# A hybrid decoder trunk on one core: PSUM evictions of the FFN groups at a higher scheduling priority, three of four joined blocks written back one product later

## The chip, the cores and the metric

The kernel runs on one core of a Trainium2 chip. The metric is device time in microseconds (us) of the whole program, from one launch; three runs of the kernel before give a median of 2379.33 us (2377.66 to 2384.99). A profile of one execution gives the times of single instructions. The engines have short names in it: PE is TensorE (matmul), PEld its weight load, DVE is VectorE, ACT is ScalarE, POOL is GpSimd, SP is SyncE, whose queue starts the DMAs.

## The reference

Two layers (DEPTH = 2) act on x of 512 tokens by 1024 features. Each layer is a half-step SwiGLU FFN, a mixing block of three gated branches (stick-breaking attention, forgetting attention, memory cross-attention), and a second half-step FFN, each with an RMS norm before and after. All is float32. The change touches the FFN alone:

```python
def _swiglu(t, w_gate, w_up, w_down):
    return (jax.nn.silu(t @ w_gate) * (t @ w_up)) @ w_down

f = _swiglu(_rmsnorm(h, ffn1_pre_g[l]), ffn1_w_gate[l], ffn1_w_up[l], ffn1_w_down[l])
h = h + 0.5 * _rmsnorm(f, ffn1_post_g[l])
...
f = _swiglu(_rmsnorm(h, ffn2_pre_g[l]), ffn2_w_gate[l], ffn2_w_up[l], ffn2_w_down[l])
h = h + 0.5 * _rmsnorm(f, ffn2_post_g[l])
```

The hidden width D_FF is 2816, that is 22 tiles of 128.

## The kernel before, in words

**Stages.** The program runs FFN a0, mixing, FFN c0 (layer 0), then FFN a1, mixing, FFN c1 (layer 1). Names of tiles carry these letters: `pwa0g` is a PSUM bank of the token-major gate products of a0, `pdc` one of the down products of c0 or c1, `wh_da` a weight of the down group of a0 or a1.

**Three matmuls for one.** A float32 operand is kept as an upper part and a rest (`h` and `l`); `split` (line 179) makes the upper part by a copy on ACT (line 182, or 185 with a scale) and the rest by a subtraction on DVE (line 183 or 186). `mm3` (line 203) adds three matmuls into one bank: upper by upper (205), upper by rest (206), rest by upper (207). Each weight tile thus needs a DMA into a `raw` tile, a cast on ACT and a subtraction on DVE before PE can use it. The tiles `wh` and `wl` have four buffers each (`BUFS`, line 102), and a product of the groups below uses two of each.

**Seven products for eight.** Sixteen of the 22 hidden tiles are computed token-major, in two column halves `ci` = 0 and 1, in groups of seven products in place of eight block products (a Winograd form of Strassen's scheme). `token_product` (line 740) is one such product of gate or up; the groups are called G0, U0, G1 and U1 here. Weights of the seven products are blocks or differences of blocks of the weight (`BlockUnit`, line 274; the difference is made on DVE at line 327). The products run in `ORDER` (0, 2, 1, 3, 4, 5, 6). `SUM` says into which of three pairs of PSUM banks a product adds: pair 0 takes products 0, 3, 5 and 6, pair 1 takes 1, pair 2 takes 2 and 4. Pair 1 starts as a copy of pair 0 after product 0 (line 747). A pair is read between the products that add to it, and a product may add to its pair only when the reading before it is done; products 5 and 6 follow each other directly on pair 0.

**Reading out.** At the end of a product its two banks are read: copies on ACT for products 2 and 3 (line 775), additions on DVE for 4 and 5 (line 777), for 1 and 6 a multiplication by the gate on DVE in the up groups (line 779) or a Silu on ACT in the gate groups (line 781). After 4 and 5 follow a product of whole tiles on DVE (line 784) or a Silu on ACT (line 786).

**Joined blocks.** After products 1, 4, 5 and 6 of an up group one block of the hidden tensor is ready, but token-major; the down group needs it the other way round. `turns` (line 788) collects these blocks, and `turn` (line 790), called four times in each later product, works on them: in the first product after, two copies of 16-bit halves on ACT (line 800) and two transposing DMAs on SP (line 801); when the block has age 2, two copies on ACT (line 804) join the halves in the hidden tensor. The blocks of products 1 and 5 take their planes from the tag `rs`, which has one buffer, the others from the five temporaries (line 99).

**The down group.** `product` (line 851) runs fourteen products of the same kind in the order `DOWN` (line 849), for both column halves into the same banks, so that they are read only after the second half (lines 875 to 886; line 878 copies pair 0 to pair 1). Each factor on the left is made one product ahead by `first_factor` (line 829) from the joined blocks. Eight plain gate and up products of the hidden tiles 18 to 21 stand between the down products (`PLAN`, line 1643).

**What sets the order.** The jobs form a queue (`Queue`); when a job begins, the weights of the jobs after it are loaded and split, four units ahead (`load_ahead`, line 391; a product has two units), so splits stand early in the program. A scheduler of the language then orders the instructions of each engine: among those that it reckons ready when an engine falls free, it takes the one with the best priority, which without further word is its place in the program. On the chip every engine works through its own list in that order.

Of the kernel before, what the change touches and what calls it, by code (L numbers as in the profile page):

```python
# [13 lines left out]
AF = mybir.ActivationFunctionType  # L14
ALU = mybir.AluOpType
# [8 lines left out]
def kernel(  # L24
# [38 lines left out]
    nc = tc.nc  # L63
# [35 lines left out]
    def tmp(name):  # L99
        return sb.tile([P, S], F32, tag="f32t", bufs=5, name=name)  # L100
# [3 lines left out]
    def stile(shape, tag, name, dt=F32R):  # L104
        return sb.tile(shape, dt, tag=tag, bufs=BUFS[tag], name=name)
# [4 lines left out]
    def pbank(tag, name):  # L110
        return ps.tile([P, S], F32, tag=tag, bufs=4, name=name)
# [91 lines left out]
    def mm3(pt, lh, ll, rh, rl, start, stop, free=False):  # L203

        nc.tensor.matmul(pt, lh, rh, start=start, stop=False, skip_group_check=free)  # L205
        nc.tensor.matmul(pt, lh, rl, start=False, stop=False, skip_group_check=free)  # L206
        nc.tensor.matmul(pt, ll, rh, start=False, stop=stop, skip_group_check=free)  # L207
# [261 lines left out]
    HF = (slice(0, S), slice(S, D))  # L469
# [128 lines left out]
    ORDER = (0, 2, 1, 3, 4, 5, 6)  # L598
    SUM = (0, 1, 2, 0, 2, 0, 0)
    TO = ((0, 0), (0, 0), (1, 1), (0, 1), (0, 1), (1, 1), (1, 0))  # L600
    park = [nc.dram_tensor(f"park{i}", (NT, P, D), F32, kind="Internal").ap() for i in range(2 * L)]

    def ffn(l, src, wg, wu, wd, dst, name, spare, parked, plan, aside=None):
# [6 lines left out]
        hid, st = {}, {}  # L610
        hr, turns = {}, []
# [122 lines left out]
        def in_product(n):  # L734
            if n in (0, 1, 6):
                i, j = ((0, 0), (0, 1), None, None, None, None, (1, 1))[n]
                return [block(i, j, part) for part in range(2)]
            return st["u", n]

        def token_product(ci, up, n, uns):  # L740

            nm = f"{name}{'gu'[up]}_{ci}_{n}"
            if n in (0, 1, 2):
                st["c", n] = [pbank("z" if n == 0 else "mm", f"pw{nm}_{e}") for e in range(2)]
            if n == 1:
                for e in range(2):
                    nc.scalar.copy(st["c", 1][e][:], st["c", 0][e][:])
            if n == 0:
                if not up:
                    st["s", ci] = {}  # L750
            pts = st["c", SUM[n]]
            h, l = in_product(n)
            opens, ends = n in (0, 2), n in (1, 4, 6)
            for un in uns:
                for e in range(2):
                    c = slice(e * P, (e + 1) * P)
                    for k in range(un.nk):
# [12 lines left out]
            r = hidden_rows(2 * ci + q[1])[:, :, HALVES[q[0]]] if up else g  # L770
            for e in range(2):
                p = pts[e][:].rearrange("p (f q) -> p f q", f=2)
                re, ge = r[:, 2 * e:2 * e + 2], g[:, 2 * e:2 * e + 2]
                if n in (2, 3):
                    nc.scalar.copy(re, p)
                elif n in (4, 5):
                    nc.vector.tensor_tensor(re, re, p, ALU.add)
                elif up:
                    nc.vector.tensor_tensor(ge, p, ge, ALU.mult)
                else:  # L780
                    nc.scalar.activation(re, p, AF.Silu)
            if n in (4, 5):
                if up:
                    nc.vector.tensor_tensor(g, r, g, ALU.mult)
                else:
                    nc.scalar.activation(r, r, AF.Silu)
            if up and n in (1, 4, 5, 6):
                turns.append([nm, g, (2 * ci + q[1], q[0]), n in (1, 5), 0, None])

        def turn(kk):  # L790

            for one in turns:
                nm, g, (row, i), own, age, planes = one
                if kk == 1 and age == 0:
                    one[5] = planes = ([stile([P, 2, 2 * S], "rs", "tr" + nm, U16)[:, h] for h in range(2)] if own else
                                       [tmp(f"tr{nm}_{h}")[:].bitcast(U16) for h in range(2)])
                    words = g.rearrange("p f q -> p (f q)").bitcast(U16)
                    for h, plane in enumerate(planes):
                        part = tmp(f"th{nm}_{h}")[:].bitcast(U16)
                        nc.scalar.copy(part, words[:, h::2])  # L800
                        nc.sync.dma_start_transpose(plane.rearrange("p (r q) -> p r q", q=P), part)
                if kk in (0, 1) and age == 2:
                    r = hidden_rows(row)[:].bitcast(U16)
                    nc.scalar.copy(r[:, :, i * S + kk:(i + 1) * S:2].rearrange("p f (e q) -> p e f q", e=2),
                                   planes[kk].rearrange("p (e f q) -> p e f q", e=2, q=P))
                if kk == ND // 2 - 1:
                    one[4] += 1
            turns[:] = [one for one in turns if one[4] < 3]

        def token_products(ci, up):  # L810

# [39 lines left out]
        def product(at, uns):  # L851
            ci, n = DOWN[at]
            first, last = ci == 0, ci == NC - 1
            if at == 0:
                RINGS["o"] = 2
                dst.begin()
            if at + 1 < len(DOWN):
                first_factor(*DOWN[at + 1])
            if first and n in (0, 2):
                st["b", SUM[n]] = [pbank("z", f"pd{name}_{n}_{e}") for e in range(2)]  # L860
            pts = st["b", SUM[n]]
            h, l = st.pop(("a", ci, n))
# [12 lines left out]
            if n == 0:  # L875
                st["b", 1] = [pbank("z", f"pd{name}_1_{e}") for e in range(2)]
                for e in range(2):
                    nc.scalar.copy(st["b", 1][e][:], pts[e][:])
                return
            i, hf = TO[n]  # L880
            for e in range(2):
                f = dst.fs[2 * i + e][:, HF[hf]]
                if n in (4, 5):
                    nc.vector.tensor_tensor(f, f, pts[e][:], ALU.add)
                else:
                    nc.scalar.copy(f, pts[e][:])

        def products():

# [768 lines left out]
    for l in LAYERS:  # L1658
        i, mn = 3 * l, []
# [44 lines left out]
```

## Time and profile before

| | us |
|---|---|
| median of three runs | 2379.33 |
| lowest and highest run | 2377.66, 2384.99 |
| the profiled execution, its time | 2378.89 |
| its span in the profile | 2377.2 |
| DVE busy | 1805.5 (76%) |
| ACT busy | 1515.2 (64%) |
| PE, granted clock over the span | 0.999 of full |

The profiled execution lies 0.44 us below the median, and 1.7 us of its time lie outside the span. "Busy" of PE includes time in which a matmul that has begun is drawn out; the ends of matmuls are modelled. A row of the timeline gives the start, the duration, the engine, the line of the kernel, the operation, the tiles written and read, the shape, and in brackets the idle time of the engine just before with what ended it. A row of the waits gives the engine and line that waited, whom it waited for, and the us in total, the times and the longest.

### The profile page before, as it was taken

The numbers are of one execution on the slowest core, as the hardware profiler recorded it, in microseconds if no ns is written. First come the engines' busy times: TensorE is split into PE (matmuls) and PEld (weight loads), VectorE is DVE, ScalarE is ACT, GpSimd is POOL, SyncE is SP. The second block draws the span as 40 slices with busy tenths as digits, with TensorE's granted clock in tenths as the row PEclk, the third lists the DMA queues.
The fourth block names the chain that finished last, engine by engine and source line by source line (L and its number), as shares of the span: only waits on it lengthen the run. The fifth ranks groups of instructions, "written<-read, shape, count | busy, mean of one in ns | idle before, by whom it ended". The sixth has DMA issues, their size and how long they took to land.

```text
span 2377.2 us, 31155 instructions
## 1 busy us (share of the span) xinstructions
PE 2348.8 (99%) x11719; PEld 1982.8 (83%) x11719; DVE 1805.5 (76%) x2358; ACT 1515.2 (64%) x2306; POOL 76.0 (3%) x134
## 2 busy tenths in 40 slices
PE   9999999999999999999999999999999999999998
PEld 7777889888888888778888878888888888887787
DVE  8876877667777689778788778766777767897785
ACT  6777565577766556775557665655777664666744
POOL 0000000000111000000000000000001100000000
PEclk9999999999999999999999999999999999999999
DMA  5666455223223556664647664532323235576643
GB/s 199 194 176 182 159 190 151 75 81 94 86 75 107 186 178 177 185 186 142 230 134 208 182 177 161 199 110 71 98 72 98 80 116 200 160 203 171 194 145 141
DMA packets 299754, 354.98 MB, mean 149 GB/s; under 512 B 78266, under 2 KB 192978, under 8 KB 299604
## 3 DMA queue, kind: packets, MB, share of 16 engines
q1 hardware_dynamic: 299508, 352.97, 48.3%
q8 instruction: 92, 1.51, 0.3%
q14 instruction: 58, 0.48, 0.1%
q0 software_dynamic: 96, 0.03, 0.0%
HBM read 319.39 MB, written 16.78 MB: 141 GB/s over the span
## 4 chain that ended last, share of the span: by engine, by line
PE 84%; DVE 5%; DMA 5%; ACT 4%; issue 2%; SPq 0%; POOL 0%; DVEq 0%; ACTq 0%
PE pg L206 4%; PE pg L205 4%; PE pg L207 4%; PE pda L206 2%; PE pda L207 2%; PE pdc L206 2%; PE pda L205 2%; PE pdc L207 2%; PE pdc L205 2%; PE pb L207 1%; PE pb L206 1%; PE pb L205 1%; DMA raw_da<-in_ffn_w_down_dram 1%; PE pq L206 1%; PE pq L205 1%
## 5 line engine op out<-in xcount | busy, mean ns | idle before, releaser
L205 PE MATMUL pg<-us_a,wh_wg 128*128 128x512 f32 x384 | 150.9, 393 | 0.0
L207 PE MATMUL pg<-us_a,wl_wg 128*128 128x512 f32 x384 | 149.8, 390 | 0.0
L206 PE MATMUL pg<-us_a,wh_wg 128*128 128x512 f32 x384 | 149.8, 390 | 0.0
L206 PE MATMUL pda<-wl_da,aha 128*128 128x512 f32 x224 | 87.8, 392 | 3.5 <-DVE wl_da L183 3.5
L206 PE MATMUL pdc<-wl_dc,ahc 128*128 128x512 f32 x224 | 87.9, 392 | 3.0 <-DVE wl_dc L183 3.0
L205 PE MATMUL pdc<-wh_dc,ahc 128*128 128x512 f32 x224 | 86.8, 390 | 1.4 <-ACT wh_dc L182 1.3
L205 PE MATMUL pda<-wh_da,aha 128*128 128x512 f32 x224 | 86.7, 390 | 1.1 <-ACT wh_da L182 1.1
L207 PE MATMUL pdc<-wh_dc,alc 128*128 128x512 f32 x224 | 87.2, 389 | 0.0
L207 PE MATMUL pda<-wh_da,ala 128*128 128x512 f32 x224 | 87.2, 389 | 0.0
L183 DVE TENSOR_TENSOR wl_da<-raw_da,wh_da 128x1024 fp32r<-128x1024 f32 x50 | 60.9, 1223 | 34.3 <-ACT wh_da L182 34.3
L207 PEld LDWEIGHTS pg<-us_a,wl_wg 128*128 128x128 f32 x384 | 72.1, 188 | 15.2
L183 DVE TENSOR_TENSOR wl_dc<-raw_dc,wh_dc 128x1024 fp32r<-128x1024 f32 x50 | 61.0, 1222 | 30.5 <-ACT wh_dc L182 30.4
L205 PEld LDWEIGHTS pg<-us_a,wh_wg 128*128 128x128 f32 x384 | 72.1, 188 | 14.1
L206 PEld LDWEIGHTS pg<-us_a,wh_wg 128*128 128x128 f32 x384 | 72.2, 188 | 14.1
L182 ACT CAST wh_da<-raw_da 128x1024 fp32r<-128x1024 f32 x50 | 52.2, 1050 | 47.0 <-PE pda L207 16.6
L182 ACT CAST wh_dc<-raw_dc 128x1024 fp32r<-128x1024 f32 x50 | 52.3, 1050 | 43.5 <-PE pdc L207 17.6
L186 DVE SCALAR_TENSOR_TENSOR wl_wg<-raw_wg,wh_wg 128x1024 fp32r<-128x1024 f32 x48 | 58.4, 1220 | 22.2 <-ACT wh_wg L185 22.2
L200 DVE SCALAR_TENSOR_TENSOR ga<-pg,bgate,ga 128x512 f32<-128x512 f32 x48 | 35.9, 747 | 50.0 <-ACT ga L199 50.0
L185 ACT ACTIVATE wh_wg<-raw_wg 128x1024 fp32r<-128x1024 f32 x48 | 50.6, 1058 | 24.7 <-PE pv L1096 11.7
L183 DVE TENSOR_TENSOR wl_uc<-raw_uc,wh_uc 128x1024 fp32r<-128x1024 f32 x44 | 53.7, 1220 | 16.5 <-ACT wh_uc L182 16.5
L182 ACT CAST wh_uc<-raw_uc 128x1024 fp32r<-128x1024 f32 x44 | 46.1, 1050 | 30.7 <-PE pgc L206 7.6
L183 DVE TENSOR_TENSOR wl_ua<-raw_ua,wh_ua 128x1024 fp32r<-128x1024 f32 x44 | 53.6, 1219 | 15.0 <-ACT wh_ua L182 15.0
(647 smaller groups left out, 8053.7 us busy)
## 6 DMA issues: line engine op xcount, KB each, us to landing
raw_da<-in_ffn_w_down_dram SPq DMA_DIRECT2D x66, 512.0 KB, 4.4
raw_dc<-in_ffn_w_down_dram SPq DMA_DIRECT2D x66, 512.0 KB, 4.2
raw_ga<-in_ffn_w_gate_dram SPq DMA_DIRECT2D x52, 512.0 KB, 4.3
raw_ua<-in_ffn_w_up_dram SPq DMA_DIRECT2D x52, 512.0 KB, 4.4
raw_gc<-in_ffn_w_gate_dram SPq DMA_DIRECT2D x52, 512.0 KB, 4.1
raw_uc<-in_ffn_w_up_dram SPq DMA_DIRECT2D x52, 512.0 KB, 3.6
raw_wg<-in_w_gate_dram SPq DMA_DIRECT2D x48, 512.0 KB, 3.5
raw_wo<-in_w_out_dram SPq DMA_DIRECT2D x24, 512.0 KB, 3.4
```

The source lines that it names most:

```text
L182: both = [nc.scalar.copy(h_ap, src)]
L183: make = lambda: nc.vector.tensor_tensor(l_ap, src, h_ap.bitcast(F32), ALU.subtract)
L185: both = [nc.scalar.activation(h_ap, src, AF.Copy, scale=scale)]
L186: make = lambda: nc.vector.scalar_tensor_tensor(l_ap, src, scale, h_ap.bitcast(F32), ALU.mult, ALU.subtract)
L200: nc.vector.scalar_tensor_tensor(t, z, minus, t, ALU.max, ALU.add)
L205: nc.tensor.matmul(pt, lh, rh, start=start, stop=False, skip_group_check=free)
L206: nc.tensor.matmul(pt, lh, rl, start=False, stop=False, skip_group_check=free)
L207: nc.tensor.matmul(pt, ll, rh, start=False, stop=stop, skip_group_check=free)
```

## The change

Three things are edited. The instructions that read PSUM in `token_product` and in `product` are traced inside `tc.high_priority(offset=300)`, which moves their priority 300 places ahead of their place in the program. A block that waits to be joined carries an age of its own, `back`: 2 for the second of the four blocks in ORDER (product 4), 3 for the others (products 1, 5 and 6), where it was 2 for all. Which blocks take their planes from `rs` is now written by their place in ORDER; these are products 1 and 5 as before.

```diff
             if n == 1:
                 for e in range(2):
+                  with tc.high_priority(offset=300):
                     nc.scalar.copy(st["c", 1][e][:], st["c", 0][e][:])
...
-            for e in range(2):
-                p = pts[e][:].rearrange("p (f q) -> p f q", f=2)
...
+            with tc.high_priority(offset=300):
+                for e in range(2):
+                    p = pts[e][:].rearrange("p (f q) -> p f q", f=2)
+                    re, ge = r[:, 2 * e:2 * e + 2], g[:, 2 * e:2 * e + 2]
+                    if n in (2, 3):
+                        nc.scalar.copy(re, p)
+                    elif n in (4, 5):
+                        nc.vector.tensor_tensor(re, re, p, ALU.add)
+                    elif up:
+                        nc.vector.tensor_tensor(ge, p, ge, ALU.mult)
+                    else:
+                        nc.scalar.activation(re, p, AF.Silu)
+                if n in (4, 5):
+                    if up:
+                        nc.vector.tensor_tensor(g, r, g, ALU.mult)
+                    else:
+                        nc.scalar.activation(r, r, AF.Silu)
             if up and n in (1, 4, 5, 6):
-                turns.append([nm, g, (2 * ci + q[1], q[0]), n in (1, 5), 0, None])
+                at = [n for n in ORDER if n in (1, 4, 5, 6)].index(n)
+                turns.append([nm, g, (2 * ci + q[1], q[0]), at % 2 == 0, 0, None, 2 if at == 1 else 3])
...
-                nm, g, (row, i), own, age, planes = one
+                nm, g, (row, i), own, age, planes, back = one
...
-                if kk in (0, 1) and age == 2:
+                if kk in (0, 1) and age == back:
...
-            turns[:] = [one for one in turns if one[4] < 3]
+            turns[:] = [one for one in turns if one[4] <= one[6]]
...
+            with tc.high_priority(offset=300):
+                if n == 0:
+                    st["b", 1] = [pbank("z", f"pd{name}_1_{e}") for e in range(2)]
+                    for e in range(2):
+                        nc.scalar.copy(st["b", 1][e][:], pts[e][:])
+                    return
+                i, hf = TO[n]
                 for e in range(2):
-                    nc.scalar.copy(st["b", 1][e][:], pts[e][:])
-                return
-            i, hf = TO[n]
-            for e in range(2):
-                f = dst.fs[2 * i + e][:, HF[hf]]
-                if n in (4, 5):
-                    nc.vector.tensor_tensor(f, f, pts[e][:], ALU.add)
-                else:
-                    nc.scalar.copy(f, pts[e][:])
+                    f = dst.fs[2 * i + e][:, HF[hf]]
+                    if n in (4, 5):
+                        nc.vector.tensor_tensor(f, f, pts[e][:], ALU.add)
+                    else:
+                        nc.scalar.copy(f, pts[e][:])
```

More of the change, by code (lines that the diff above doesn't have):

```diff
@@ L770, in token_product @@
             r = hidden_rows(2 * ci + q[1])[:, :, HALVES[q[0]]] if up else g
-            for e in range(2):
-                p = pts[e][:].rearrange("p (f q) -> p f q", f=2)
[L773 to L779, printed above, removed]
-                else:
-                    nc.scalar.activation(re, p, AF.Silu)
-            if n in (4, 5):
[L783 to L786, printed above, removed]
+            with tc.high_priority(offset=300):
[15 more added lines that the diff above has]
+                        nc.scalar.activation(r, r, AF.Silu)
             if up and n in (1, 4, 5, 6):
-                turns.append([nm, g, (2 * ci + q[1], q[0]), n in (1, 5), 0, None])
+                at = [n for n in ORDER if n in (1, 4, 5, 6)].index(n)
+                turns.append([nm, g, (2 * ci + q[1], q[0]), at % 2 == 0, 0, None, 2 if at == 1 else 3])
         def turn(kk):
             for one in turns:
-                nm, g, (row, i), own, age, planes = one
+                nm, g, (row, i), own, age, planes, back = one
                 if kk == 1 and age == 0:
@@ L874, in product @@
                 return
-            if n == 0:
-                st["b", 1] = [pbank("z", f"pd{name}_1_{e}") for e in range(2)]
-                for e in range(2):
-                    nc.scalar.copy(st["b", 1][e][:], pts[e][:])
-                return
-            i, hf = TO[n]
-            for e in range(2):
-                f = dst.fs[2 * i + e][:, HF[hf]]
-                if n in (4, 5):
-                    nc.vector.tensor_tensor(f, f, pts[e][:], ALU.add)
-                else:
-                    nc.scalar.copy(f, pts[e][:])
+            with tc.high_priority(offset=300):
[5 more added lines that the diff above has]
+                i, hf = TO[n]
+                for e in range(2):
+                    f = dst.fs[2 * i + e][:, HF[hf]]
[3 more added lines that the diff above has]
+                        nc.scalar.copy(f, pts[e][:])
         def products():
```

## The prediction

> **What bounds the kernel now.** I read the page's first part, then the waits of PE, then the timelines of PE, DVE and ACT around the longest waits.
>
> ```profile
> span 2377.2 us, 31155 instructions
> ...
> PE   9999999999999999999999999999999999999998
> ```
>
> PE is busy for 2348.8 of 2377.2 us, so 28.4 us of the span is all that any reordering can win. The change touches the token-major groups and the down group of the four FFN stages. Four windows hold these (60 to 330, 880 to 1200, 1218 to 1525 and 2055 to 2345 us); their sum row:
>
> ```profile
> sum 1187.00, PE 1169.84 PEld 959.67 DVE 945.91 ACT 767.29 POOL 5.39; mean PE 292.46 PEld 239.92 DVE 236.48 ACT 191.82 POOL 1.35
> ```
>
> In them PE is not busy for 1187.00 - 1169.84 = 17.2 us. That is the ceiling, 0.7% of the time. The waits of PE say whom it waits for (us in total, times, longest):
>
> ```profile
> PE pda L206 <- DVE wl_da L183: 3.5, 4, 1.3
> PE pdc L206 <- DVE wl_dc L183: 3.0, 4, 0.8
> PE pwa0u L205 <- ACT wh_ga L182: 2.0, 1, 2.0
> PE pdc L205 <- ACT wh_dc L182: 1.3, 1, 1.3
> PE pda L205 <- ACT wh_da L182: 1.1, 1, 1.1
> PE pwc1u L206 <- DVE wl_uc L183: 0.8, 1, 0.8
> PE pwa0u L206 <- DVE wl_ua L183: 0.8, 1, 0.8
> PE pwa1u L206 <- DVE wl_ua L183: 0.6, 1, 0.6
> PE pwa0u L205 <- ACT wh_ua L182: 0.5, 1, 0.5
> PE pwc1u L205 <- ACT wh_uc L182: 0.5, 1, 0.5
> PE pwc0u L206 <- DVE wl_uc L183: 0.4, 1, 0.4
> ```
>
> The reader is to see what is missing as much as what is there. Nearly all of it is a wait for a weight: L182 makes the upper part `wh` on ACT, L183 the lower part `wl` on DVE. An eviction out of PSUM hardly appears by name. These eleven rows make 14.5 us. To see why weights are late I went to where it happens. In the first FFN stage, at the end of the second gate group (G1):
>
> ```profile
> 151.68 0.39 PE L207 MATMUL pwa0g<-wh_ga,ula 128*128 128x512 f32 x1
> 152.58 0.50 PE L205 MATMUL pwa0u<-wh_ua,us_x 128*128 128x512 f32 x1 [0.51 <-ACT wh_ua L182]
> ...
> 154.43 0.50 PE L205 MATMUL pwa0g<-wh_ga,us_x 128*128 128x512 f32 x1
> ```
>
> The row at 151.68 is the last matmul of G1's product 5. The next one should belong to product 6 (`pwa0g`), but PE turns to two matmuls of the next group (`pwa0u`), whose weight is not there, and comes to product 6 at 154.43. Products 5 and 6 use the same pair of banks (SUM is 0 for both) and stand next to each other in ORDER, so product 6 may start only when line 777 has read product 5 out. The scheduler found that eviction later than the end of product 5 and filled the hole with work that on the chip is late. What DVE did:
>
> ```profile
> 150.41 1.22 DVE L183 TENSOR_TENSOR wl_ga<-tga,wh_ga 128x1024 fp32r<-128x1024 f32 x1
> 152.56 1.22 DVE L183 TENSOR_TENSOR wl_ua<-raw_ua,wh_ua 128x1024 fp32r<-128x1024 f32 x1 [0.93 <-ACT wh_ua L182]
> 153.70 1.28 DVE L777 TENSOR_TENSOR sa<-sa,pwa0g 128x512 f32<-128x512 f32 x2
> ```
>
> After `wl_ga` it idles 0.93 us for the next weight, splits it, and only then evicts, although product 5 ended at 151.9. **The wait is written on a weight; its root is the eviction's place in DVE's order.** The same at the end of U1, where the down group follows:
>
> ```profile
> 190.62 0.39 PE L207 MATMUL pwa0u<-wh_ua,ula 128*128 128x512 f32 x1
> ...
> 191.98 0.39 PE L207 MATMUL pwa0u<-wh_ua,ula 128*128 128x512 f32 x1
> 193.49 0.49 PE L205 MATMUL pda<-wh_da,aha 128*128 128x512 f32 x1 [1.12 <-ACT wh_da L182]
> ...
> 195.55 0.40 PE L205 MATMUL pwa0u<-wh_ua,us_x 128*128 128x512 f32 x1
> ```
>
> ```profile
> 192.26 1.22 DVE L183 TENSOR_TENSOR ala<-hra,aha 128x1024 fp32r<-128x1024 f32 x1
> 193.47 1.23 DVE L183 TENSOR_TENSOR wl_da<-raw_da,wh_da 128x1024 fp32r<-128x1024 f32 x1
> 194.61 1.28 DVE L777 TENSOR_TENSOR hra<-hra,pwa0u 128x512 f32<-128x512 f32 x2
> ```
>
> Six matmuls lie between the starts 190.62 and 191.98: 0.227 us each, so 24 make a product of 5.44 us.
>
> **The change part by part.** It adds and removes no instruction. The evictions of lines 747, 775 to 786 and 878 to 886 get a better place when the scheduler has several ready instructions for one engine. It can't take one that isn't ready.
>
> (a) End of U1, four times. Product 5 ends at 191.98 + 0.23 = 192.21 and product 6 starts at 195.55 with four matmuls of the down group (0.91 us) between: 2.43 us lost. If line 777 takes the place of `wl_da` at 193.47, its first half (0.64 of 1.28 us) is done at 194.11, and 1.90 us are lost. Gain 0.53, four times: 2.1 us. The split that is pushed back serves the down group, which now starts a product (5.44 us) later; that covers its 1.28 us. Were the cover gone, it would cost these 1.28 us each time.
>
> (b) End of G1, four times. Product 5 ends at 151.91, product 6 starts at 154.43, two matmuls (0.45) lie between: 2.07 us lost. With line 777 right after `wl_ga`, at 150.41 + 1.14 (1.14 is the step from 193.47 to 194.61), product 6 starts at about 152.2 and loses 0.3 us: gain 1.7. The rows of the waits for U groups (0.8, 0.8, 0.6, 0.5, 0.5, 0.4) make 3.6 us, this place 0.51 + 0.8 of it, so all four gain 1.7 x 3.6 / 1.3 = 4.7 us. That needs an eviction that is ready when DVE falls free. Two slipped matmuls, 0.45 us, say that the scheduler saw it less than one DVE operation late: perhaps it wasn't ready, and then priority does nothing. Bounds 0 and 4.7; I take two thirds, 3.1, as four slipped matmuls at (a) show that being taken late for want of priority is common.
>
> (c) End of U0 in layer 0, where PE waited for line 777 behind a split:
>
> ```profile
> 110.88 0.39 PE L207 MATMUL pwa0u<-wh_ua,ula 128*128 128x512 f32 x1
> 113.24 0.47 PE L205 MATMUL pwa0u<-wh_ua,us_x 128*128 128x512 f32 x1 [1.97 <-ACT wh_ga L182]
> ```
>
> ```profile
> 111.27 1.22 DVE L183 TENSOR_TENSOR wl_ua<-tua,wh_ua 128x1024 fp32r<-128x1024 f32 x1 [0.37 <-ACT wh_ua L182]
> ```
>
> If line 777 stands where `wl_ua` stands, its first half ends at 111.27 + 0.64 = 111.91 against a start of product 6 at 113.24: gain 1.3. The row names ACT, which ended last by the profile. Bounds 0 (the order stays) and 2.1 (no wait at all: 113.24 - 110.88 - 0.23); I take 1.3.
>
> (d) The clock. In c1, the last FFN stage, the hand-over of (b) is followed by a drop:
>
> ```profile
> 150.00:160.00 10.00, 8.63 (x36) 6.36 (x35) 6.51 (x8) 5.65 (x6) 0.00 (x0) 1.00 0.80 255
> 2168.00:2176.00 8.00, 7.14 (x22) 5.31 (x23) 3.89 (x5) 3.12 (x4) 0.00 (x0) 0.79 0.69 211
> ```
>
> At a granted 0.79 over 8 us, PE lost some 0.21 x 8 = 1.7 us; after the same stall in the first stage the clock stayed at 1.00. Bounds 0 and 1.7; I take half, 0.8. [...]
>
> (e) The joins (line 804). Three of four blocks per up group come one product later in the program: 8 groups x 3 x 2 copies. None is added. What they cost now is that they stand in ACT's order while their transfer is in flight:
>
> ```profile
> 183.80 1.35 ACT L804 COPY hra<-tra0u 128x1024 uint16<-128x1024 uint16 x1 [2.87 <-DMA tra0u<-tha0u]
> ...
> 185.96 0.58 ACT L775 COPY hra<-pwa0u 128x512 f32<-128x512 f32 x1
> ```
>
> ```profile
> ACT hrc L804 <- DMA trc0u<-thc0u: 9.0, 6, 2.1
> ```
>
> The copy at 183.80 held ACT for 2.87 us, with casts and an eviction behind it. But it runs in product 4, while the program has it in product 5: the scheduler takes a join as soon as its own reckoning says that the data is there. A later place in the program need not move it, so I take 0. Bounds: if it moves, the weights of the hand-overs come earlier, up to what (a) and (c) leave, (4 x 1.90) + 0.8 = 8.4 us; if it hurts, see the third rival. The first joined block of U1 (product 1) is needed by the second down product, two products (10.9 us) after product 6 begins; moved from product 5 to product 6 it keeps about one product of cover, which would cost up to 5.44 us if it were gone. The tag `rs` has one buffer and line 795 makes a tile of it for each plane, so an own block's second transpose waits for its first join, and SP's loads queue behind that transpose.
>
> (f) The down group's own waits:
>
> ```profile
> 223.13 0.50 PE L206 MATMUL pda<-wl_da,aha 128*128 128x512 f32 x1 [0.63 <-DVE wl_da L183]
> ...
> 1062.49 0.50 PE L206 MATMUL pdc<-wl_dc,ahc 128*128 128x512 f32 x1 [0.67 <-DVE wl_dc L183]
> ...
> 1399.52 0.50 PE L206 MATMUL pda<-wl_da,aha 128*128 128x512 f32 x1 [1.31 <-DVE wl_da L183]
> ...
> 2239.25 0.50 PE L206 MATMUL pdc<-wl_dc,ahc 128*128 128x512 f32 x1 [0.82 <-DVE wl_dc L183]
> ```
>
> 3.4 us together. They follow loads and joins, not evictions: 0 taken, bounds -3.4 and +3.4.
>
> Sum: 2.1 + 3.1 + 1.3 + 0.8 = 7.3 us. The profiled execution took 2378.89 us (span 2377.2 and 1.7 around it), 0.44 below the median 2379.33. 2378.9 - 7.3 = **2371.6 us**, 0.32% below the median.
>
> **The rivals.** First, **nothing moves**. For it: the scheduler takes what is ready, so a priority decides only ties; two slipped matmuls at (b) fit an eviction that wasn't ready, and the join at 183.80 floats. Against: four slipped at (a). Time: 2378.9, or 2376.8 with (a) alone.
>
> Second, **evictions block weights**, the slower case. ACT takes its work in order, as the row at 183.80 shows. An eviction put ahead of a cast waits for its matmul, and if PE on the chip runs later than the scheduler reckoned, the cast waits with it. The price is two halves of line 775 (0.58 us each), 1.16 us, at every place where PE already waits for a weight: three hand-overs and one down place in each of four stages, 16 x 1.16 = 18.6 us: 2397.5; at half of the places 2388.2. It decides once the cast stands ready before the eviction's matmul has ended. For it: PE waits for casts by name. Against: between hand-overs PE shows no wait, so there a cast has slack. [...]
>
> Third, **joins come too late**: SP's transposes move with them, the loads behind too, and the waits of (f) double: 2378.9 + 3.4 = 2382.3.
>
> **How the numbers follow.** A run of this kernel can be told from no change at about 0.3%, 7.1 us, that is below 2372.2 or above 2386.5. Forecast 0.46, of which 0.03 ends inside 0.3%; nothing moves 0.30; evictions block 0.18, nearly all of it outside; joins late 0.06. So faster 0.43, same 0.39, slower 0.18. The forecast's own range is 2364 (all of (b), (c), (d) and some of (e): 2.1 + 4.7 + 2.1 + 1.7 + 4 = 14.6) to 2374. To hold 8 in 10 the range takes in the second case and a third of the blocking one: 2364 to 2387.
>
> **What would show it.** Right: at 151.9 and 192.2 of the new profile product 6 follows product 5 with at most one strange matmul between; line 777 stands ahead of `wl_ua` and `wl_da`; the rows for `pwa0u`, `pda` L205 and `pdc` L205 shrink. Wrong: two and four slipped matmuls as now (first rival); new PE rows for `wh` in the middle of a group, with line 775 ahead of the cast (second); longer rows at 223 and 1062 us (third). Joins that stand a product later with no ACT wait for `tra` or `trc` would mean that (e) was worth more than 0.

## The result and the profile after

The changed kernel takes 2385.95 us (median of 20 runs, 2380.41 to 2397.7), the kernel before beside it 2380.55 us (20 runs, 2377.13 to 2386.56). The ratio is **1.0026, 95% interval 1.0015 to 1.0037**: 0.26% slower, some 6 us, where 0.3% faster was forecast. The profiled execution took 2384.19 us with a span of 2382.5. Lines up to 746 are the same in both kernels; further down line 777 of before is 779 in the changed kernel, 784 is 786, 786 is 788, 804 is 807 and 878 is 882. ACT has one load of an activation table less (2305 instructions for 2306); the other engines have as many instructions as before.

The four FFN windows of the changed kernel, sum row (us, PE busy, and so on):

```profile
sum 1187.00, PE 1164.49 PEld 957.09 DVE 945.46 ACT 760.95 POOL 3.45; mean PE 291.12 PEld 239.27 DVE 236.37 ACT 190.24 POOL 0.86
```

PE is not busy for 22.5 us of them, 5.3 us more than the 17.2 of before. So most of the loss is idle time of PE in the FFN stages. That the span also grew by 5.3 us is partly chance: from the first gate matmul to the last down matmul the four stages took 7.0 us more (slower matmuls add 1.9 us, see (d)), and the rest of the program took 1.8 us less in this execution. The waits of PE, the largest first:

```profile
PE pwa0u L205 <- DVE hra L779: 4.6, 3, 2.1
PE pdc L206 <- DVE wl_dc L183: 4.5, 2, 2.4
PE pda L206 <- DVE wl_da L183: 3.1, 2, 1.9
PE pwc0u L205 <- DVE hrc L779: 1.7, 2, 1.4
PE pwc1u L205 <- DVE hrc L779: 1.6, 1, 1.6
...
PE pwa1u L205 <- DVE hra L779: 1.2, 2, 1.1
```

Two things changed against the list of before. The eviction now stands there by name (line 779), in the place of the waits for `wh_da` and `wh_dc` at the end of U1, and of the wait for `wh_ga` at the end of U0 in a0, which is 2.1 of the 4.6 us. And the rows for `wl_da` and `wl_dc`, which were 3.5 and 3.0 us in eight waits, are 3.1 and 4.5 us in four: the four waits at the end of U1 are gone from them, and the four of step (f) grew from 3.4 to 7.6 us.

The end of U1 in the first stage, PE and then DVE:

```profile
191.83 0.39 PE L207 MATMUL pwa0u<-wh_ua,ula 128*128 128x512 f32 x1
194.32 0.47 PE L205 MATMUL pwa0u<-wh_ua,us_x 128*128 128x512 f32 x1 [2.10 <-DVE hra L779]
```

```profile
192.36 1.22 DVE L183 TENSOR_TENSOR ala<-hra,aha 128x1024 fp32r<-128x1024 f32 x1
193.49 0.68 DVE L779 TENSOR_TENSOR hra<-hra,pwa0u 128x512 f32<-128x512 f32 x1
194.09 1.22 DVE L183 TENSOR_TENSOR wl_da<-raw_da,wh_da 128x1024 fp32r<-128x1024 f32 x1
195.22 0.68 DVE L779 TENSOR_TENSOR hra<-hra,pwa0u 128x512 f32<-128x512 f32 x1
```

Line 779 took the place of `wl_da` at 193.49, as step (a) had it, and the four slipped matmuls are gone in all four stages. But product 5 ended at 192.06, and DVE still makes the left factor `ala` first; the second half of the eviction waits behind `wl_da`. Lost at this place is 194.32 - 192.06 = 2.26 us, against 2.43 before.

The end of G1:

```profile
151.89 0.39 PE L207 MATMUL pwa0g<-wh_ga,ula 128*128 128x512 f32 x1
152.40 0.49 PE L205 MATMUL pwa0u<-wh_ua,us_x 128*128 128x512 f32 x1
...
154.26 0.50 PE L205 MATMUL pwa0g<-wh_ga,us_x 128*128 128x512 f32 x1
```

Two matmuls still slip in, here and in the other three stages: the order at this place did not change. The joins float as before, and ACT still waits inside products 4 and 5 for their transfers:

```profile
184.39 1.35 ACT L807 COPY hra<-tra0u 128x1024 uint16<-128x1024 uint16 x1 [1.48 <-DMA tra0u<-tha0u]
...
188.91 1.37 ACT L807 COPY hra<-tra0u 128x1024 uint16<-128x1024 uint16 x1 [2.27 <-DMA tra0u<-tha0u]
```

What ends late in the down group is a load. DVE in the last stage, before and then changed; line 327 makes the difference of two blocks, from which the weight of the waiting matmul is split:

```profile
2233.80 1.23 DVE L327 TENSOR_TENSOR btc<-btc,raw_dc 128x1024 f32<-128x1024 f32 x1 [2.26 <-DMA raw_dc<-in_ffn_w_down_dram]
2236.84 1.22 DVE L327 TENSOR_TENSOR btc<-btc,raw_dc 128x1024 f32<-128x1024 f32 x1 [1.81 <-DMA raw_dc<-in_ffn_w_down_dram]
```

```profile
2238.11 1.23 DVE L327 TENSOR_TENSOR btc<-btc,raw_dc 128x1024 f32<-128x1024 f32 x1 [2.49 <-DMA raw_dc<-in_ffn_w_down_dram]
2242.12 1.22 DVE L327 TENSOR_TENSOR btc<-btc,raw_dc 128x1024 f32<-128x1024 f32 x1 [2.78 <-DMA raw_dc<-in_ffn_w_down_dram]
```

DVE waited for these loads before, too; it now waits longer, and the wait of PE behind the second of them grew from 0.82 to 2.43 us.

### The profile page after: what moved, and what is told of

Read it like the earlier page. It is cut to its first block, busy times and chain, and to the rows that moved or that the text cites. A ratio compares the mean times of both kernels' runs of the same rounds, so it can differ in the third digit from the quotient of the medians.

```text
span 2382.5 us, 31148 instructions
## 1 busy us (share of the span) xinstructions
PE 2348.3 (99%) x11719; PEld 1983.8 (83%) x11719; DVE 1805.5 (76%) x2358; ACT 1512.8 (63%) x2305; POOL 73.4 (3%) x134
## 4 chain that ended last, share of the span: by engine, by line
PE 87%; DVE 4%; ACT 3%; DMA 3%; issue 2%; SPq 0%; POOL 0%; DVEq 0%; ACTq 0%
PE pg L206 3%; PE pg L205 3%; PE pg L207 3%; PE pdc L206 3%; PE pdc L207 3%; PE pdc L205 3%; PE pda L206 2%; PE pda L207 2%; PE pda L205 2%; PE pb L206 2%; PE pb L207 2%; PE pb L205 2%; PE pwo L206 1%; PE pq L206 1%; PE pq L205 1%
## 5 line engine op out<-in xcount | busy, mean ns | idle before, releaser
L183 DVE TENSOR_TENSOR wl_da<-raw_da,wh_da 128x1024 fp32r<-128x1024 f32 x50 | 60.9, 1223 | 30.8 <-ACT wh_da L182 30.5
L185 ACT ACTIVATE wh_wg<-raw_wg 128x1024 fp32r<-128x1024 f32 x48 | 50.5, 1057 | 25.0 <-PE pv L1100 11.7
```

The source lines that it names most:

```text
L183: make = lambda: nc.vector.tensor_tensor(l_ap, src, h_ap.bitcast(F32), ALU.subtract)
L185: both = [nc.scalar.activation(h_ap, src, AF.Copy, scale=scale)]
```

## The experiments

The first theory (A) was that the priority in the down group makes the loss; the rivals were the priority in the token-major groups (B) and the later joins (C). Ratios below are against runs of the kernel before on the same chip, each with its 95% interval. "Down waits" are the sum over the four stages of the wait of step (f), from the timelines of PE of the one profiled execution.

### Four parts, each by itself

All evictions keep the priority, the joins go back:

```diff
-                turns.append([nm, g, (2 * ci + q[1], q[0]), at % 2 == 0, 0, None, 2 if at == 1 else 3])
+                turns.append([nm, g, (2 * ci + q[1], q[0]), at % 2 == 0, 0, None, 2])
```

> Keeps the priority of all evictions, takes back the later joins (all four blocks join two products later again). Theory A (the loss comes from the priority in the down group) and theory B (it comes from the priority in the token-major groups) both leave the joins out of it: the time of the changed kernel, +0.2 to +0.3% against before (2384 to 2388 us), and the same rows of TensorE's waits. Theory C (the later joins cost the time): within 0.1% of before.

Measured: 1.0018 (1.0007 to 1.0029). The order of instructions came out the same as the changed kernel's on every engine, so this is a second measurement of that order.

Only the later joins (the edit in all three places):

```diff
-            with tc.high_priority(offset=300):
+            with ExitStack():
```

> Only the later joins, no priority. Theories A and B: no cost; one join of each stage goes behind the two copies of the down accumulator on ScalarE, so that the first weight tile of the down group's second product may come up to 0.8 us earlier in a stage: 0 to -3 us, ratio 0.9987 to 1.000. Theory C: +0.2 to +0.3%.

Measured: 0.9992 (0.9979 to 1.0004), down waits of at most 0.8 us in each stage. C falls.

Priority in the token-major groups alone (`ExitStack()` in the down group, joins back):

> Priority only for the evictions of the token-major groups, joins as before. Theory A: within 0.1% of before, the four slipped matmuls at the end of U1 gone, PE waiting on the evictions there instead, and the down group's own weight waits near 3.4 us in all as in before. Theory B: +0.2 to +0.3% as the changed kernel, with the down group's weight waits near 7.5 us in all.

Measured: 1.0005 (0.9992 to 1.0018). The down waits were 6.6 us in all, not the 3.4 that A expected here.

Priority in the down group alone (`ExitStack()` in `token_product`, joins back):

> Priority only for the evictions of the down group, joins as before. Theory A: +0.2 to +0.3%, the four waits of the down group on the first weight tiles of its second product near 7.5 us in all instead of 3.4. Theory B: within 0.1% of before and these waits near 3.4 us.

Measured: 1.0018 (1.0006 to 1.0031), down waits 7.4 us. A fits the times.

### The copies of line 882, or the rest of the down group

The priority puts the two copies from pair 0 to pair 1 ahead of the casts of the next down weights. ACT in the last stage, changed kernel:

```profile
2231.31 0.61 ACT L882 COPY pdc<-pdc 128x512 f32<-128x512 f32 x1
2231.86 1.04 ACT L182 CAST wh_dc<-raw_dc 128x1024 fp32r<-128x1024 f32 x1
2232.80 0.58 ACT L882 COPY pdc<-pdc 128x512 f32<-128x512 f32 x1
2233.32 1.04 ACT L182 CAST wh_dc<-raw_dc 128x1024 fp32r<-128x1024 f32 x1
2234.27 1.36 ACT L807 COPY hrc<-trc1u 128x1024 uint16<-128x1024 uint16 x1
```

Until a cast and its split are done, the tile that they read isn't free for the next load: in the changed profile SP waited 20 times for a split of `wl_da` and 19 times for one of `wl_dc` before a load (line 249), 68.2 and 67.8 us in all. So the first copy, 0.55 us, could delay the load on which PE waits. Two kernels part it. The copies alone (`ExitStack()` in `token_product`, joins back):

```diff
-            with tc.high_priority(offset=300):
+            with tc.high_priority(offset=300) if n == 0 else ExitStack():
```

> Priority only for the two copies of the down accumulator from pair 0 to pair 1 (line 882), nothing else of the change. Theory A1 (these copies go ahead of the casts of the first two weights of the next down product, 0.55 us each, so the load behind those weights starts later): +0.15 to +0.25% (2389.5 to 2392 us against 2385.8 of before), down weight waits of 6.5 to 8 us in all. Theory A2 (the loss is in the other reads of the down group and in the left factors that move with them): within 0.1% of before, waits near 3.4 us.

Measured: 1.0001 (0.9990 to 1.0013), down waits 4.4 us.

All of the change but the copies:

```diff
-            with tc.high_priority(offset=300):
+            with ExitStack() if n == 0 else tc.high_priority(offset=300):
```

> The whole change with its later joins, but without priority for the two copies of line 882. Theory A1: within 0.1% of before, down weight waits of 3 to 4.5 us in all. Theory A2: +0.15 to +0.25%, as the changed kernel.

Measured: 1.0001 (0.9989 to 1.0013), down waits 6.6 us. Neither the copies alone nor everything but the copies shows the loss; both theories fail on one of the two.

Beside them, an edit aside from the change: an own block takes one `rs` tile for both planes. First without the change, then with the priority in the token-major groups.

```diff
-                    one[5] = planes = ([stile([P, 2, 2 * S], "rs", "tr" + nm, U16)[:, h] for h in range(2)] if own else
+                    one[5] = planes = ([t[:, h] for t in [stile([P, 2, 2 * S], "rs", "tr" + nm, U16)] for h in range(2)] if own else
```

> Without the change; an own block takes one tile of the tag rs for both planes in place of one for each, so that its second transpose no longer waits for its first join. If the loads behind that transpose set the waits of the down group, they fall from 3.4 to under 2 us and ScalarE's waits for the joins of products 1 and 5 shrink: -0.05 to -0.2%. If the copies of line 882 alone matter: within 0.1% of before.

Measured: 1.0003 (0.9993 to 1.0013). The hoped-for fall of the down waits did not come (6.0 us).

> The one tile for both planes together with priority for the evictions of the token-major groups alone. If the priority there is held back by VectorE being behind (which the earlier joins should lift), the waits for line 779 at the end of U1 fall from 1.0 to 2.1 us to under 1: -0.1 to -0.3% against before. Otherwise within 0.1%.

Measured: 1.0009 (0.9997 to 1.0020), no gain, down waits 4.1 us. That the joins of products 1 and 5 wait for each other costs nothing that these runs can tell from no change.

### Dose, and the rest of the down group alone

Priority for the reads of the down group but the copies (the edit above, with `ExitStack()` in `token_product` and the joins back):

> Priority for the reads of the down group except the two copies of line 882, nothing else of the change. Together with the kernel that gave priority to all of the down group (+0.18%) and the one that gave it to the copies alone (+0.01%). If the rest of the down group carries the loss: +0.1 to +0.25%. If the loss needs the copies and the rest together, or is the copies' alone and was missed within the interval: within 0.1%.

Measured: 0.9993 (0.9980 to 1.0007), down waits 5.2 us. The rest of the down group alone shows no cost.

Each copy of line 882 twice (`range(2)`), and then four times, with the priority for the copies alone and without any:

```diff
-                        nc.scalar.copy(st["b", 1][e][:], pts[e][:])
+                        for _ in range(4):
+                            nc.scalar.copy(st["b", 1][e][:], pts[e][:])
```

> Priority for the copies of line 882 alone, and each copy made twice (the second writes the same again). If a copy ahead of the casts delays the weights of the next down product by its own 0.55 us or more: +0.1 to +0.3% against before and at least 0.1% over the kernel with the same doubled copies without priority; down weight waits of 6 to 10 us in all. If the copies have cover: within 0.1% of before and of that kernel.

> No part of the change; the copies of line 882 made twice, at their old place behind the casts. It shows what the doubled copies cost there: within 0.1% of before by every theory, as ScalarE has a hole of about 1 us behind them.

Measured: twice with priority 1.0017 (1.0002 to 1.0031), down waits 6.4 us; twice without 0.9990 (0.9979 to 1.0001), down waits 2.4 us. That spoke for the copies.

> Priority for the copies of line 882 alone, each made four times: six more copies of 0.55 us stand ahead of the cast of the second weight tile of the next down product. If the place of the copies ahead of that cast is the loss: 4 stages x 6 x 0.55 us = 13 us less what cover there is: +0.3 to +0.55% against before, and 0.2% or more over the same kernel without priority. If they have cover: within 0.1% of that kernel.

> No part of the change; the copies of line 882 made four times at their old place behind the casts (the last of them writes the same as the first). 4 stages x 6 x 0.55 us = 13 us of more work on ScalarE, which waits some 4 us there in the profile of before: within 0.15% of before if the place, not the work, makes the loss; +0.3% or more if the work does.

Measured: four times with priority 1.0001 (0.9989 to 1.0014), down waits 2.3 us; four times without 1.0013 (1.0001 to 1.0026), down waits 0.5 us. **Six more copies ahead of the second cast show no cost, so the dose speaks against the copies.** With the copies made once (1.0001) it fits that by themselves they have cover; the pair with two copies does not fit it.

### The end of U1

The left factor of the second down product may not stand ahead of the eviction; then the split of the first down weight may not either. All of them are on DVE, and the dependency is one without a semaphore:

```diff
                     elif n in (4, 5):
                         nc.vector.tensor_tensor(re, re, p, ALU.add)
+                        st["read"] = nc.cur_bb.bb.instructions[-1].name
...
             split(h, l, src)
+            if (ci, n) == (1, 0):
+                nosync = mybir.DependencyInfo(mybir.DependencyClass.NoSync, mybir.DependencyReason.DATA)
+                tc.add_manual_dep(nc.cur_bb.bb.instructions[-1], st["read"], nosync, reason="in_order")
```

> Priority for the evictions of the token-major groups alone, and the lower part of the left factor of the second down product (line 183 for al) may not stand ahead of the reading of product 5 of the second up group. If VectorE being busy with that factor when product 5 ends is why the priority gained nothing there: TensorE's waits for line 779 at the end of the second up group fall from 1.0 to 2.1 us to below 1.0 in each stage, 2 to 5 us in all, -0.1 to -0.2% against before. If something else takes the place (the split of the down weight): the waits stay above 1 us and the time within 0.1%.

Measured: 0.9993 (0.9979 to 1.0006), down waits 3.9 us. The wait went from the first bank to the second, and what took its place is named by DVE, where `ala` no longer stands ahead of line 779 and line 779 is now split by `wl_da` alone (its halves at 195.61 and 198.45 us, `wl_da` at 197.31):

```profile
195.42 0.39 PE L207 MATMUL pwa0u<-wh_ua,ula 128*128 128x512 f32 x1
196.44 0.47 PE L205 MATMUL pwa0u<-wh_ua,us_x 128*128 128x512 f32 x1 [0.63 <-ACT tha0u L804]
...
199.19 0.50 PE L205 MATMUL pwa0u<-wh_ua,us_x 128*128 128x512 f32 x1 [1.12 <-DVE hra L779]
```

With the weight held back too (the same dependency for the split of the first unit of the first down product):

> Priority for the evictions of the token-major groups alone; at the end of the second up group the left factor of the second down product and the split of the first down weight on VectorE may both stand only behind the two halves of line 779. If the place of these two in VectorE's order is the root of the wait there: TensorE's waits for line 779 at that place shrink to below 0.7 us in each stage, without a new wait in the down group, 3 to 6 us in all: -0.1 to -0.25% against before. If the gain is given back later: within 0.1%, with longer waits on the first weights of the down group.

Measured: 0.9996 (0.9983 to 1.0009). PE at the same place, and PE's waits for the lower down weights:

```profile
193.16 0.39 PE L207 MATMUL pwa0u<-wh_ua,ula 128*128 128x512 f32 x1
194.23 0.47 PE L205 MATMUL pwa0u<-wh_ua,us_x 128*128 128x512 f32 x1 [0.69 <-ACT tha0u L811]
```

```profile
PE pda L206 <- DVE wl_da L183: 4.8, 2, 2.9
PE pdc L206 <- DVE wl_dc L183: 3.5, 2, 2.2
```

DVE has both halves of the eviction from 193.41 us on, `wl_da` at 195.10 and `ala` at 198.52. At the end of U1 only 194.23 - 193.39 = 0.84 us are lost now, 2.35 us in the four stages together, and no wait there is put down to the eviction any more (line 781 in this kernel; the copy on ACT that the row names ended within about 0.1 us of the eviction's first half). But the down waits are 8.3 us, where the token-major priority alone had 6.6. **The gain at U1 is there, and some 30 us later PE waits longer for a load.** From product 5's last matmul, PE reaches the waiting matmul of step (f) 0.36 us earlier per stage than with the token-major priority alone (29.29 after 29.65 us, means of the four stages), and starts it 0.09 us later (31.38 after 31.29). These are one profile of each. The time does not settle it: the interval reaches down to 0.9983, 4 us below the kernel before, so a good part of the 4.5 us gained at U1 (6.9 to 2.35, see the table below) may have been kept.

### How far one profile may be trusted, and the change once more

All edits switched off:

> No part of the change (the edits stand in the text of the kernel, all switched off), so the order of before on every engine. Every theory: within 0.1% of before. Its profile is a second look at that order, on the chip of these runs: the down weight waits of the first look were 3.4 us in all; if this look gives 2.5 to 4.5 us, single looks may be compared; if it gives 6 us or more, they may not.

Measured: 1.0004 (0.9991 to 1.0018). Its waits:

```profile
PE pdc L206 <- DVE wl_dc L183: 4.7, 4, 2.0
PE pda L206 <- DVE wl_da L183: 4.2, 4, 1.4
```

Four of the eight are the waits at the end of U1, 0.76 us each as in before, so its down waits are 5.8 us where the first profile of the same order gave 3.4. That lies between the two limits set beforehand (4.5 and 6), close to the upper one: one profile does not settle a difference of 4 us in these waits. Several must be taken together.

The changed kernel again, and beside it the one without priority for the copies:

> The changed kernel as it is, beside the next kernel on the same chip. If the priority of the copies of line 882 is what makes the loss in this surrounding: +0.15 to +0.3% against before, and 0.1% or more over the next kernel. If the loss was an accident of single builds and chips: within 0.1% of before.

> The changed kernel without priority for the copies of line 882 (the two of the first accumulator go behind the cast of the first weight tile again). If these copies make the loss in this surrounding: within 0.1% of before and 0.1% or more below the changed kernel beside it. If they do not: the same ratio as the changed kernel, +0.1 to +0.25%.

Measured: the changed kernel 1.0018 (1.0005 to 1.0032), without the copies' priority 1.0011 (0.9999 to 1.0022). The difference, 0.07%, decides nothing by itself. With the earlier runs the changed order stands at 1.0026, 1.0018 and 1.0018 (mean 1.0021, 5.0 us of 2383), the one without the copies' priority at 1.0001 and 1.0011 (mean 1.0006).

PE's waits in the other two profiles of the changed order, first the one with the joins back:

```profile
PE pda L206 <- DVE wl_da L183: 6.5, 2, 4.1
PE pdc L206 <- DVE wl_dc L183: 5.2, 2, 2.8
```

```profile
PE pda L206 <- DVE wl_da L183: 5.6, 2, 3.6
...
PE pdc L206 <- DVE wl_dc L183: 3.6, 2, 1.9
```

So its down waits were 7.6, 11.7 and 9.2 us.

## Why the prediction was wrong, by its own steps

The kernels run differ only in a few places, so their profiles can be taken together for each place. The time lost at a hand-over is the step from the start of product 5's last matmul to the start of product 6's first, less 0.227 us for that matmul and for each one slipped in between, summed over the four stages. Ten profiles have no priority in the token-major groups (before, control, joins, down group, rest of it, copies alone, twice and four times, with and without), six have it and nothing held back. The two kernels with one `rs` tile for both planes are left out.

| us lost, four stages | before, control | changed order, three profiles | mean of 10 without | mean of 6 with | gain | forecast |
|---|---|---|---|---|---|---|
| (a) end of U1 | 7.7, 10.1 | 6.7, 7.4, 7.2 | 9.1 | 6.9 | 2.2 | 2.1 |
| (b) end of G1 | 6.3, 4.3 | 7.8, 10.7, 8.3 | 6.4 | 9.0 | -2.6 | 3.1 |
| (c) end of U0 | 2.6, 3.1 | 2.3, 2.8, 2.2 | 3.3 | 2.4 | 0.9 | 1.3 |
| end of G0, last three stages | 0.8, 0.8 | 0, 0, 0 | 0.8 | 0 | 0.8 | not seen |

The standard error of a mean is 0.3 us in (a), 0.4 and 0.5 in (b) and 0.2 in (c). The table compares executions on different chips, so it carries sizes and not the single cause.

(a) **Right in size.** 2.2 us were gained of 2.1. The first two profiles alone (7.7 to 6.7) hid half of it. The two kernels that hold work back show that DVE's order was indeed the root, and that about 4.5 us more lay there (6.9 to 2.35).

(b) **The first step that failed.** The bound was 0 because "perhaps it wasn't ready, and then priority does nothing". The order bears that out: it is unchanged at that place, and two matmuls slip as before (when the scheduler reckoned the eviction ready is not on record). But the time lost there did not stay, it grew by 2.6 us, and no bound below zero had been set. One way there can be read in c0, where the loss grew most between the first two profiles (0.92 to 2.55 us; a1 1.19 to 2.22, while a0 fell from 2.08 to 1.69 and c1 from 2.07 to 1.36). ACT in the kernel before, then ACT in the changed one, and DVE before and changed:

```profile
989.70 1.06 ACT L786 ACTIVATE sc<-sc 128x1024 f32<-128x1024 f32 x1 [1.65 <-DVE sc L777]
990.67 1.03 ACT L182 CAST wh_uc<-raw_uc 128x1024 fp32r<-128x1024 f32 x1
```

```profile
991.98 1.06 ACT L788 ACTIVATE sc<-sc 128x1024 f32<-128x1024 f32 x1 [3.28 <-DVE sc L779]
992.94 1.98 ACT L182 CAST wh_uc<-raw_uc 128x1024 fp32r<-128x1024 f32 x2
```

```profile
982.70 1.23 DVE L327 TENSOR_TENSOR tuc<-tuc,raw_uc 128x1024 f32<-128x1024 f32 x1 [3.09 <-DMA tuc<-in_ffn_w_up_dram]
```

```profile
984.98 1.23 DVE L327 TENSOR_TENSOR tuc<-tuc,raw_uc 128x1024 f32<-128x1024 f32 x1 [3.23 <-DMA tuc<-in_ffn_w_up_dram]
...
990.66 1.28 DVE L779 TENSOR_TENSOR sc<-sc,pwc0g 128x512 f32<-128x512 f32 x2
```

The cast of the weight that PE wants next stands behind a Silu on ACT, the Silu behind an eviction on DVE, and that one behind a difference of blocks, for whose load DVE sat idle for 3.23 us. DVE sat idle for the same load before, 3.09 us, but there the wait ended 2.28 us earlier. The last matmul of product 5, before and changed:

```profile
992.01 0.39 PE L207 MATMUL pwc0g<-wh_gc,ulc 128*128 128x512 f32 x1
```

```profile
992.65 0.39 PE L207 MATMUL pwc0g<-wh_gc,ulc 128*128 128x512 f32 x1
```

It came 0.64 us later, the cast 2.27 us later. PE arrives, and the chain behind the load isn't done. Why the load came later was not tried and stays open. SP's order changed at one place in each stage: a transpose of the block of product 1 goes ahead of one gate load. In c0 that is at 945 us. A gate load 9 us behind it leaves at 954.47 us in place of 953.84, 0.63 us later, no more than PE itself is late; the load in question leaves 1.86 us later (980.08 after 978.22). So that place alone does not explain it.

(c) Half right: 0.9 us, 0.45 of it in a0 (2.74 to 2.29), where all of 1.3 had been expected.

(d) **Wrong in sign.** The drop in c1 is gone from the changed profile (granted 1.00 over 2168 to 2176 us, where it was 0.79), but others came. After the longest wait of c0 and ahead of the longest of c1, stretch, us, PE, PEld, DVE, ACT and POOL busy, granted clock:

```profile
1065.50:1069.50 4.00, 4.00 (x12) 3.15 (x11) 4.00 (x4) 0.15 (x1) 0.00 (x0) 0.57 0.79 254
2236.00:2242.00 6.00, 6.00 (x27) 4.71 (x26) 1.23 (x1) 2.38 (x4) 0.00 (x0) 1.00 0.89 301
```

At 0.57 over 4 us, 1.7 us are lost on top of a wait of 2.0. In the three profiles of the changed order such stretches cost 7.3, 9.4 and 6.5 us in all, in the two of before 5.4 and 6.8 (the excess over 0.227 us of all steps of 0.33 to 0.58 us between two matmuls of the FFN stages without a wait of more than 0.15 us before the second): 1.6 us more on average, where 0.8 less was forecast.

(e) Right: the joins float. Taken back, the order of the changed kernel did not alter; alone, they show no cost.

(f) **The second step that failed: taken at 0, it was the largest term.** The down waits are 9.5 us in the mean of the three profiles of the changed order and 4.6 in the two of before, 4.9 us more where the bounds were -3.4 and +3.4; without the copies' priority 6.6 and 5.2, with the token-major priority alone 6.6. The reasoning, "they follow loads and joins, not evictions", named what PE waits for and drew the wrong end from it. A wait for a load grows when PE comes earlier, and when the weight comes later. Both happened, by these five profiles: from product 5's last matmul in U1, PE reached the waiting matmul (the 123rd after it) after 30.0 and 31.0 us in the two of before, means of the four stages, and after 30.3, 30.1 and 30.0 us in the changed order; the weight let it start after 30.8 and 32.5, and after 32.2, 33.0 and 32.3 us. So 4 x 0.36 = 1.4 us come from PE being earlier, and 4 x 0.85 = 3.4 us from the weight being later. What made the weight later is not shown, and the two profiles of before lie 1.6 us apart in it.

The sum over the places for the changed order: -2.2 + 2.6 - 0.9 - 0.8 + (9.5 - 4.6) = 3.6 us, and with the slower matmuls of (d) 1.6 us more: 5.2, against 5.0 measured. That this is so close is luck. Its terms come from different sets of profiles and are each uncertain by 1 us or more. From the five profiles of the two orders alone it is -1.8 + 3.7 - 0.4 - 0.8 + 4.9 + 1.6 = 7.2 us, where the four FFN stages of the same profiles, 1266.5 us for 1257.3 on average, lie 9.1 us apart (7.0 of it waits of PE).

**The rivals.** The first fails, things moved at three hand-overs. The second had the sign, but not the mechanism: in the down group the first cast stands behind 0.55 us of a copy, not behind 1.16 us of line 775 (777 in the changed kernel) at half of the places, and that copy alone shows no cost; PE's waits for casts in the token-major groups (1.0 and 0.7 us) stand at the end of G1, none in the middle of a group. The third gave 2382.3, and (f) did more than double, but not through the joins.

**What stays open.** Priority in all of the down group cost 0.18%, its two halves -0.07% and 0.01%; twice the copies cost 0.17%, four times 0.01%. These don't add up to one culprit. Five pairs of kernels differ in the priority of the copies alone: with it the ratio is higher by 0.15% (the means of the changed order and of the one without), 0.25% (the whole down group and its rest), 0.01% (the copies once) and 0.27% (twice), and lower by 0.12% (four times). Their mean is 0.11%, so the copies are not cleared, but the pairs differ among themselves by more than that. Nor do the down waits alone set the time: they were 6.6 and 8.3 us in kernels at 1.0005 and 0.9996, and 0.5 us in one at 1.0013. The reading that is left is that the down group's load chain is at its limit and small delays that meet there add to one another, and that is argued, not shown. None of the kernels beats the one before by more than its interval.

## What to carry to other kernels

A gain at one hand-over can be lost at the next place where the same engine waits for a load. Before counting it, look for that place, and ask of its wait both when the engine will come and when the load will: here that wait grew by 4.9 us, and by these profiles the later weight was the larger part. Put a bound below zero on every step that leaves an order unchanged, since its arrival times can change all the same: at (b) the order stayed and the loss grew by 2.6 us. Where one order gives waits of 3.4 and 5.8 us in two executions, take several profiles before a difference of a few us is explained.

## What the runs showed of the hardware

TensorE's clock dropped after some short waits here and not after others: in the changed kernel 0.57 was granted over 4 us behind the wait of 2.02 us in c0, 1.00 over 4 us behind that of 2.43 us in c1. Of the waits of 0.4 us or more in the FFN stages of all twenty profiles, those of 2.5 us or longer were followed by a stretch at about half pace (a matmul every 0.43 us in place of 0.227; at least three such steps within 5 us) in 19 of 24 cases, at a mean cost of 1.5 us; those of 2.0 to 2.5 us in 13 of 25, those below 2 us in 58 of 315. Of these 58, 55 had another wait of 0.4 us or more within 8 us before or after; of the 257 without a slow stretch 107 had. So here several short waits close together went with such a stretch too. The longest wait, 4.07 us, in the changed order with the joins back:

```profile
227.60:231.60 4.00, 3.92 (x9) 3.14 (x10) 4.00 (x5) 0.00 (x0) 0.00 (x0) 0.50 0.65 207
```

The granted clock is 0.50 over the 4 us that follow. A wait of 2.5 us or longer thus mostly cost some 1.5 us more than its own length, as the 19 of 24 cases show.
